# A two-layer decoder trunk on one core: a refitted table of transfer durations and a larger delay for the inverse in the ordering pass, and the S5 tables loaded in two transfers

## The chip, the core and the metric
The kernel runs on one core of one Trainium2 chip. The metric is the device time of one execution in microseconds. "PE" is the matrix engine, "DVE" the vector engine, "ACT" the scalar engine, "POOL" GpSimd, and "SP" the engine that issues most DMA transfers here.

## The reference
A decoder trunk of two post-norm layers on x (1024 positions, 1024 features), in fp32, with 256 memory tokens:
```python
for i in range(2):
    if i == 0:
        mix, xq = gdn_mixer(x, ...)      # gated DeltaNet, 8 heads of 128
    else:
        mix, xq = s5_mixer(x, ...)       # 64 groups, 64 complex states each, GLU
    cross = memory_attention(xq, mem, w_kv[i])          # 4 heads
    h = concatenate([mix, cross], -1) @ w_o[i]
    x = layer_norm(ALPHA * x + h, ln1_g[i], ln1_b[i])
    f = square(relu(x @ mlp_w1[i])) @ mlp_w2[i]         # 1024 -> 4096 -> 1024
    x = layer_norm(ALPHA * x + f, ln2_g[i], ln2_b[i])
```
In the DeltaNet, each chunk of 64 positions solves a unit triangular system (I + A) X = [V, K exp(g)], where A is the strictly lower part of beta K K^T times a decay. Then a state S of 128 x 128 per head goes from chunk to chunk: v_new = u - w S, o = (q exp(g)) S + (q k^T decay) v_new, S = S exp(g_last) + k_dec^T v_new. The S5 mixer runs, per group, a complex diagonal recurrence over the positions.

## The kernel before
**Products.** Large products are made as three matmuls in the type fp32r (`mm3`, L386 to L391): each operand is split into a high part (a cast on ACT, L368 or L857) and a low part (a subtraction on DVE, L369 or L858). A result tile in a trace row is named after its use: wi and wz are projections of the input with xT (x, transposed) and the weights wih, wil (or wzh, wzl), loaded raw as wir (wzr) by L359. Raw weight tiles have the tag "raw", of which there are two buffers; `mlp_sums` (L626 to L637) shares them: it loads two blocks of the MLP's first weight (w1r), makes sums and differences of their quarters in place on DVE (L631 to L634) and stores them to wsum in DRAM (L636).

**Layer 0.** Heads are taken one after the other. `gdn_recur` (L1441) runs the recurrence of a head over eight steps of 128 positions: on PE, ks (L1465) and po (L1468) read S; DVE makes R (L1467); PE makes pe (L1471) from R and the inverse iv; ACT copies it to e (L1473); PE makes pS (L1477) and po (L1483) from e; DVE makes the next S (L1482). Each waits for the one before, so the projections and the convolution of a later head (DVE, L1105 to L1117) are woven in as filler.

**The inverse.** The triangular systems of two heads at a time are inverted in four rounds, heads 0/1 to 6/7. `gdn_inverse_` (L1189) inverts small blocks on DVE with products (L1256) and sums (L1258, TENSOR_REDUCE); POOL writes the results to the DRAM tensor t32 (L1268, L1269), a row of the trace named t<-X. `gdn_invert_tiles` (L1271) reads them back through SP, as iv<-t (L1292) and bd<-t (L1295), and completes the inverse with small products on PE (L1279). `self.patient` holds the names of all instructions that `gdn_inverse_` emits.

**After the heads.** `rows` (L2315) loads x for the residual in sixteen DMAs, as y (L2321); then come the output projection, the layer norm (L519, L531), the MLP, and layer 1. S5's `s5_driving` (L2005) loads, per block and half, two table tiles "tab" of [128, 4, 128] on POOL's queue (L2016); `s5_drive` multiplies them at L2059.

**Order.** The kernel is emitted in a plain order and then re-ordered as a whole by `settle` (L58 ff.), a list scheduler over all instructions of PE, ACT, DVE, POOL and SP. It holds a model of time: `price` (L295) gives each instruction how long its engine is busy and how long until its result is there. For a DMA it also gives `moves`, the time on a single modelled DMA server that serves all transfers one after the other; it depends on the size and on k, the shortest contiguous run of either side in bytes (L309, L310). Each PE instruction's due time is its place in PE's own program; for the others it is counted back from those that wait for them (L185 to L190). An instruction of DVE in `self.patient` gets a later due time (L191 to L193), so that others may go ahead of it. Among the instructions that are ready, the earliest due goes first. So a change of a price moves instructions on all engines. The order that comes out is fixed in the program; no time is decided on the chip.

Of the kernel before, what the change touches and what calls it, by code (L numbers as in the profile page):

```python
# [16 lines left out]
P = 128  # L17
# [13 lines left out]
class Trunk:  # L31
# [26 lines left out]
    def settle(self, first, last, reach=0.0, ahead=15.0, passes=1, margin=0.0, late=0.0, hold=1e3, stay=(0.0, 0.0), turn_=0.0):  # L58


        E = mybir.EngineType
# [83 lines left out]
        for x in range(n):  # L145
            for nm in uses(ins[x]) & before:
                if self.home.get(nm, "s")[0] == "ps":
                    k = nm, ins[x].engine
# [3 lines left out]
            for y in deps[x]:  # L152
                if ins[y].engine != ins[x].engine:
                    k = y, ins[x].engine
# [10 lines left out]
        for x in range(n):  # L165
            for nm in fresh[x]:
                t = held.setdefault(self.home[nm][:2], [])
# [13 lines left out]
        for _ in range(passes):  # L181
            due, now = [0.0] * n, 0.0
# [7 lines left out]
                    due[x] = min([due[y] for y in after[x] + next_[x]] + [now + 50.0]) - lag - cost[x][1]  # L190
            for x in range(n):  # L191
                if ins[x].name in self.patient and ins[x].engine == E.DVE:
                    due[x] += 15.0  # L193


            slots, turn = {}, {}
# [24 lines left out]
            while len(order) < n:  # L221
                first_ = None
                drift = free[E.PE] - due[turns[head]] if head < len(turns) else 0.0
                for e in names:
                    pick = None
                    for x in open_[e]:
# [13 lines left out]
                        k = (0, due[x] + other, r, x) if r <= free[e] + 0.1 else (1, r + other, due[x], x)  # L240
# [5 lines left out]
                r, x = first_[1:]  # L246
                e = ins[x].engine
                busy, length, moves = cost[x]
# [21 lines left out]
                for nm in fresh[x]:  # L270
                    t = self.home[nm][:2]
# [23 lines left out]
    def price(self, i, big):  # L295

        E = mybir.EngineType
        if i.opcode == "DMACopy":
            def run(ap):
                k = 1  # L300
                for s, c in reversed(ap):
                    if s != k:
                        break
                    k *= c
                return 4 * k

            q = [x.bass_ap.ap for x in (i.ins[0], i.outs[0])]
            size, k = 4e-3 * math.prod(c for s, c in q[1]), min(run(a) for a in q)
            moves = size / (300 if k >= 2048 else 230 if k >= 512 else 150 if k >= 256 else 90 if k >= 128 else 40)  # L309
            return (0.33 if i.engine != E.Pool else 0.65), 1.6 + size / 300 + (0.0 if k >= 512 else 0.7), moves  # L310
        if i.engine == E.PE:
            if i.ins[0].dtype == F32R:
                return 0.014 + 0.416e-3 * big, 0.39 if big > 256 else 0.29, 0
            wide = max(math.prod(c for s, c in x.bass_ap.ap[1:]) for x in i.ins)
            if i.is_transpose:
                return 0.11, 0.27, 0
            part = i.outs[0].bass_ap.ap[0][1] / P
            if part < 1:
                return 0.01 + 1.66e-3 * max(wide, 64) * part, 0.35, 0
            return 0.01 + 1.66e-3 * wide, 0.39, 0  # L320
        q = [x.bass_ap.ap[-1] for l in (i.ins, i.outs) for x in l if getattr(x, "bass_ap", None) is not None]
        slow = 1.65 if any(s > 1 and c > 1 for s, c in q) else 1.0
        scalars = any(math.prod(c for s, c in x.bass_ap.ap[1:]) == 1 for x in i.ins if getattr(x, "bass_ap", None) is not None) and big > 1
        if i.engine == E.Activation:
            bank = self.home.get(i.ins[0].bass_ap.tensor.name, "s")[0] == "ps"
            if i.opcode == "TensorCopy":
                t = max((0.05 if bank else 0.096) + 0.84e-3 * big * slow, 0.29)
            else:
                t = (0.08 if bank else 0.125) + 0.8e-3 * big + (0.22 if len(i.outs) > 1 else 0.0) + (0.07 if scalars else 0.0)
            return t, t + 0.1, 0  # L330
        if i.engine == E.Pool:
            t = 0.02 + 0.87e-3 * big if i.opcode == "Memset" else 0.5 if big < 2 else 1.0 if big < 8 else 0.17 + 2.1e-3 * big
            return t, 4.4 if 1 < big < 8 and i.opcode != "Memset" else t + 0.05, 0
        wide = sum(c > 1 for x in i.ins if getattr(x, "bass_ap", None) is not None for c in [math.prod(c for s, c in x.bass_ap.ap[1:])])
        if getattr(i, "is_tensor_tensor_scan", False):
            return 2.46e-3 * big, 2.46e-3 * big + 0.08, 0
        t = 0.07 + (0.53e-3 if i.opcode == "TensorScalarPtr" and wide < 2 else 1.04e-3) * big * slow + (0.06 if scalars and i.opcode == "TensorScalarPtr" else 0.0)
        return t, t + 0.08, 0
# [1666 lines left out]
    def s5_driving(self, m):  # L2005

        out = []
        for b in range(2):
            gs = slice(4 * b, 4 * b + 4)
            G1 = self.s5_load("G1", "h1", self.g1d[m, :, gs])  # L2010
            c, q = (2 * m + b) % 8, m // 4
            tabs = []
            for x in range(2):
                t = self.tile("h2", [P, 4, P], F32, "tab")
                src = self.tabd[1:3, c, q] if x else self.tabd[0, c, q].unsqueeze(0).to_broadcast([2, 64, 4, P])
                self.nc.gpsimd.dma_start(t.rearrange("p g t -> p (g t)"), src.rearrange("k p g t -> k p (g t)"))  # L2016
                tabs.append(t)
            out.append((G1, tabs))
        return out
# [462 lines left out]
```

## Time and profile before
| | |
|---|---|
| runs before | 2498.58, 2492.67, 2499.19 us; median 2498.58 |
| the profiled execution | 2495.45 us |
| its span | 2493.7 us |
| PE busy | 2461.7 us |
| mean granted clock of PE | 0.998 |
| transfers | 424.12 MB, DMA engines busy in the mean 46.2% with SP's queue and 7.3% with POOL's |

The span runs from the first to the last instruction of the profile; the rest of the execution's time lies around it. A busy PE is one with a matmul in flight: matmuls are pipelined, so a row's duration (0.39 us for 512 columns) is longer than the distance to the next row. In a timeline's row stand the start and the duration in us, the engine, line, operation, output <- input, shapes, and the count; brackets give the engine's idle time before it and what ended it. SPq is the queue side of SP. Times on POOL are rough.

### The profile page before, as it was taken

How to read it: one execution, taken by the hardware profiler on the slowest of the kernel's cores; microseconds unless marked ns; L12 is line 12 of the kernel's file. 1: busy time of each engine (PE TensorE's matmuls, PEld its weight loads, DVE VectorE, ACT ScalarE, POOL GpSimd, SP SyncE). 2: the span in 40 equal slices, each digit the busy share in tenths (PEclk: the TensorE clock that was granted, in tenths of full speed). 3: DMA queues.
4: the chain of work that ended last, by engine and by line, in shares of the span. 5: the costliest groups of instructions: out<-in, count | busy, mean ns of one | idle time of the engine just before them, and what ended most of it. 6: DMA issues, size and time to landing. Idle time of an engine off the chain costs nothing. (4 is left out here: it accounts for less than half of the span.)

```text
span 2493.7 us, 37109 instructions
## 1 busy us (share of the span) xinstructions
PE 2461.7 (99%) x12589; PEld 2043.5 (82%) x12589; DVE 1928.7 (77%) x3629; ACT 1385.4 (56%) x3091; POOL 283.7 (11%) x405
## 2 busy tenths in 40 slices
PE   9999999999999999999999999999999999999998
PEld 7888888887787888788888888888887888888886
DVE  7776868685889987879988856683988655588777
ACT  7766677755557575554444255662466555544443
POOL 1111212110001011312120122100010000000001
PEclk9999999999999999999999999999999999999999
DMA  6544445556335665587455499874137544673422
GB/s 205 130 121 147 134 142 146 167 157 209 106 125 176 212 225 182 175 281 250 140 168 158 141 247 224 206 257 153 57 124 240 176 154 152 208 275 101 148 88 98
DMA packets 292047, 424.12 MB, mean 170 GB/s; under 512 B 120032, under 2 KB 137392, under 8 KB 291856
## 3 DMA queue, kind: packets, MB, share of 16 engines
q1 hardware_dynamic: 257520, 370.40, 46.2%
q0 software_dynamic: 31744, 46.76, 7.3%
q10 hardware_dynamic: 2592, 4.59, 0.5%
q8 instruction: 99, 1.62, 0.3%
q14 instruction: 92, 0.75, 0.1%
HBM read 285.74 MB, written 135.76 MB: 169 GB/s over the span
## 5 line engine op out<-in xcount | busy, mean ns | idle before, releaser
L389 PE MATMUL q<-wkh,hkh 128*128 128x512 f32 x784 | 306.0, 390 | 0.0
L390 PE MATMUL q<-wkl,hkh 128*128 128x512 f32 x784 | 305.7, 390 | 0.0
L391 PE MATMUL q<-wkh,hkl 128*128 128x512 f32 x784 | 305.3, 389 | 0.0
L857 ACT CAST wkh<-wr 128x512 fp32r<-128x512 f32 x168 | 104.9, 624 | 238.0 <-PE q L390 156.5
L389 PEld LDWEIGHTS q<-wkh,hkh 128*128 128x128 f32 x784 | 147.2, 188 | 31.7 <-ACT wkh L857 1.0
L391 PEld LDWEIGHTS q<-wkh,hkl 128*128 128x128 f32 x784 | 147.2, 188 | 30.5
L390 PEld LDWEIGHTS q<-wkl,hkh 128*128 128x128 f32 x784 | 147.2, 188 | 30.0
L858 DVE TENSOR_TENSOR wkl<-wr,wkh 128x512 fp32r<-128x512 f32 x168 | 115.8, 689 | 64.0 <-issue 50.9
L389 PE MATMUL wi<-xTh,wih 128*128 128x512 f32 x376 | 151.8, 404 | 1.6 <-ACT wih L368 1.6
L391 PE MATMUL wi<-xTh,wil 128*128 128x512 f32 x376 | 150.0, 399 | 0.3 <-DVE wil L369 0.3
L390 PE MATMUL wi<-xTl,wih 128*128 128x512 f32 x376 | 150.1, 399 | 0.0
L512 POOL TENSOR_TENSOR mv<-mv,mhalf 128x1 f32<-128x1 f32 x32 | 32.1, 1004 | 981.0 <-DVE mv L506 936.4
L858 DVE TENSOR_TENSOR hkl<-hr,hkh 128x512 fp32r<-128x512 f32 x196 | 134.2, 685 | 2.8 <-ACT hkh L857 2.7
L857 ACT CAST hkh<-hr 128x512 fp32r<-128x512 f32 x196 | 121.3, 619 | 4.0 <-DMA hr<-hd 4.0
L389 PE MATMUL o<-ow,ok 128*128 128x512 f32 x256 | 101.4, 396 | 1.2 <-ACT ok L1733 1.0
L391 PE MATMUL o<-ow,ok 128*128 128x512 f32 x256 | 101.5, 396 | 0.2
L390 PE MATMUL o<-ow,ok 128*128 128x512 f32 x256 | 100.2, 391 | 0.1
L850 DVE TENSOR_TENSOR y<-q,y 128x512 f32<-128x512 f32 x136 | 88.0, 683 | 0.0
L389 PEld LDWEIGHTS wi<-xTh,wih 128*128 128x128 f32 x376 | 71.2, 189 | 15.2 <-ACT wih L368 1.8
L391 PEld LDWEIGHTS wi<-xTh,wil 128*128 128x128 f32 x376 | 71.2, 189 | 14.4 <-DVE wil L369 1.0
L390 PEld LDWEIGHTS wi<-xTl,wih 128*128 128x128 f32 x376 | 71.3, 190 | 12.5
L1733 ACT CAST ok<-os 128x512 fp32r<-128x512 f32 x56 | 34.8, 623 | 54.8 <-PE o L391 41.1
(619 smaller groups left out, 7287.7 us busy)
## 6 DMA issues: line engine op xcount, KB each, us to landing
hr<-hd SPq DMA_DIRECT2D x212, 256.0 KB, 2.7
wr<-in_w_dram SPq DMA_DIRECT2D x56, 512.0 KB, 5.0
hd<-u SPq DMA_DIRECT2D x100, 256.0 KB, 2.2
w1r<-in_w_dram SPq DMA_DIRECT2D x48, 512.0 KB, 3.7
hd<-hid SPq DMA_DIRECT2D x60, 256.0 KB, 2.1
hd<-p SPq DMA_DIRECT2D x60, 256.0 KB, 2.6
w1r<-in_w_dram SPq DMA_DIRECT2D x48, 256.0 KB, 3.2
wir<-in_w_in_dram SPq DMA_DIRECT2D x23, 512.0 KB, 4.3
```

Source lines behind the costliest of these rows:

```text
L389: mm(ps, a[0], b[0], start=start, stop=False, skip_group_check=onto)
L390: mm(ps, a[0], b[1], start=False, stop=False, skip_group_check=onto)
L391: mm(ps, a[1], b[0], start=False, stop=stop, skip_group_check=onto)
L512: nc.gpsimd.tensor_tensor(mv[:, 3:4], mv[:, 2:3], self.mhalf[:, 0:1], op=ALU.pow)
L850: V.tensor_tensor(o, bank[t], o, op=ALU.add)
L857: nc.scalar.copy(hi, s)
L858: nc.vector.tensor_tensor(lo, s, f32(hi), op=ALU.subtract)
L1733: nc.scalar.copy(hi, s)
```

## The change
Three edits. In `settle`, the later due time of the inverse's DVE instructions is 20 us instead of 15. In `price`, the modelled rate of a transfer by its contiguous run gets new steps: runs from 1024 bytes on count as 330 (before: 300, from 2048 on), 512 as 280 (230), 256 as 210 (150), 128 as 150 (90), 64 as 90 and shorter ones as 45 (40), and the fixed part for short runs is 0.3 us instead of 0.7. In `s5_driving`, each table tile comes in two transfers of 64 partitions instead of one of 128. The first tile's two halves are the same table, the second's are two tables that lie one behind the other.
```diff
             for x in range(n):
                 if ins[x].name in self.patient and ins[x].engine == E.DVE:
-                    due[x] += 15.0
+                    due[x] += 20.0
...
-            moves = size / (300 if k >= 2048 else 230 if k >= 512 else 150 if k >= 256 else 90 if k >= 128 else 40)
-            return (0.33 if i.engine != E.Pool else 0.65), 1.6 + size / 300 + (0.0 if k >= 512 else 0.7), moves
+            moves = size / (330 if k >= 1024 else 280 if k >= 512 else 210 if k >= 256 else 150 if k >= 128 else 90 if k >= 64 else 45)
+            return (0.33 if i.engine != E.Pool else 0.65), 1.6 + size / 330 + (0.0 if k >= 512 else 0.3), moves
...
                 t = self.tile("h2", [P, 4, P], F32, "tab")
-                src = self.tabd[1:3, c, q] if x else self.tabd[0, c, q].unsqueeze(0).to_broadcast([2, 64, 4, P])
-                self.nc.gpsimd.dma_start(t.rearrange("p g t -> p (g t)"), src.rearrange("k p g t -> k p (g t)"))
+                for k in range(2):
+                    self.nc.gpsimd.dma_start(t[64 * k:64 * k + 64], self.tabd[x * (1 + k), c, q])
                 tabs.append(t)
```
The number of instructions stays the same on PE, DVE, ACT and SP; POOL issues 32 DMAs more. The order changes mostly from 40 to 80 us (keys and values of the memory), from 150 to 620 us (the heads) and from 750 to 870 us (the layer norm), as the trace of before has these places. From there on it is nearly the same.

The first place is on PE, in the recurrence of head 6 (560 to 568 us of the trace), from pe_1091 on. pe, pS, po and ks are the recurrence's products; wi_1117 is the projection of the next head's values or keys with the weights wih_1115 and wil_1116; iv_1065 is the first product of the inverse with what came back from DRAM. Before:
```order
L1471 MATMUL pe_1091_6373<-R_1089_6360,iv_914_5420 128x128
L390 MATMUL wz_1090_6363<-xTl1_20_149,wzh_1047_6126 128x512
L391 MATMUL wz_1090_6363<-xTh1_19_148,wzl_1048_6127 128x512
L1477 MATMUL pS_1094_6396<-e_1092_6375,kdl_1002_5929 128x128
L1483 MATMUL po_1055_6170<-e_1092_6375,mix_288_1774 128x128
L1465 MATMUL ks_1098_6415<-S_1095_6398,kT_32_323 128x128
L1468 MATMUL po_1055_6170<-S_1095_6398,gb_968_5758 128x128
L1471 MATMUL pe_1101_6429<-R_1099_6417,iv_914_5420 128x128
L1483 MATMUL po_1055_6170<-e_1102_6431,mix_288_1774 128x128
L389 MATMUL wi_1117_6475<-xTh0_17_146,wih_1115_6471 128x512
L390 MATMUL wi_1117_6475<-xTl0_18_147,wih_1115_6471 128x512
L391 MATMUL wi_1117_6475<-xTh0_17_146,wil_1116_6472 128x512
```
And now, where fourteen more matmuls of wi follow, between ks, po, pe and po, before iv_1065 comes:
```order
L1471 MATMUL pe_1091_6373<-R_1089_6360,iv_914_5420 128x128
L390 MATMUL wz_1090_6363<-xTl1_20_149,wzh_1047_6126 128x512
L391 MATMUL wz_1090_6363<-xTh1_19_148,wzl_1048_6127 128x512
L389 MATMUL wi_1117_6475<-xTh0_17_146,wih_1115_6471 128x512
L390 MATMUL wi_1117_6475<-xTl0_18_147,wih_1115_6471 128x512
L1477 MATMUL pS_1094_6396<-e_1092_6375,kdl_1002_5929 128x128
L1483 MATMUL po_1055_6170<-e_1092_6375,mix_288_1774 128x128
L391 MATMUL wi_1117_6475<-xTh0_17_146,wil_1116_6472 128x512
L389 MATMUL wi_1117_6475<-xTh0_17_146,wih_1115_6471 128x512
L390 MATMUL wi_1117_6475<-xTl0_18_147,wih_1115_6471 128x512
```
The recurrence's steps stood side by side and had three matmuls of wi behind them before iv_1065; now nineteen stand between them.

The second place is SP's queue at the same time, from the storing of the sums on. Before:
```order
L2321 DMA y_1218_6991<-in_x_dram 128x512
L636 DMA wsum_125<-w1r_1105_6448 128x1024
L2321 DMA y_1219_6992<-in_x_dram 128x512
L2321 DMA y_1220_6993<-in_x_dram 128x512
L636 DMA wsum_125<-w1r_1104_6446 128x1024
L359 DMA wir_1114_6469<-in_w_in_dram 128x1024
L1353 DMA Dq_1082_6333<-ded_115 128x512
L1124 DMA gb_1083_6335<-gcd_304 128x512
L1292 DMA iv_8_107<-t32_118 32x8x32 x2
```
And now:
```order
L636 DMA wsum_125<-w1r_1105_6448 128x1024
L359 DMA wir_1114_6469<-in_w_in_dram 128x1024
L636 DMA wsum_125<-w1r_1104_6446 128x1024
L359 DMA wir_1138_6605<-in_w_in_dram 128x1024
L2321 DMA y_1218_6991<-in_x_dram 128x512
L2321 DMA y_1219_6992<-in_x_dram 128x512
L2321 DMA y_1220_6993<-in_x_dram 128x512
L1353 DMA Dq_1082_6333<-ded_115 128x512
L359 DMA wzr_1162_6736<-in_w_in_dram 128x1024
L1124 DMA gb_1083_6335<-gcd_304 128x512
L1292 DMA iv_8_107<-t32_118 32x8x32 x2
```
The weights wir and the sums moved ahead of the loads of y, and the next two raw weights ahead of the reading of the inverse.

The third place is ACT at 53 to 59 us, among the casts of the memory's value weights wvh and the scaling of keys (kd) and decays (D), as the difference of the two orders:
```order
 L368 CAST wvh_114_870<-wvr_113_868 128x1024
 L1545 CAST kv_90_725<-mk_106_806 128x256
-L368 CAST wvh_117_888<-wvr_116_886 128x1024
-L1545 CAST kv_90_725<-mk_110_839 128x256
 L1164 ACTIVATE kd_47_436<-kt_46_422,scr_5_97 128x128 x4
 L1134 ACTIVATE D_45_416<-D_45_416,scr_5_97 128x128 x4
 L1167 ACTIVATE D_45_416<-D_45_416,scr_5_97 128x128 x4
-L1179 COPY pkd_43_407<-NT_42_401 32x128
+L368 CAST wvh_117_888<-wvr_116_886 128x1024
```
One cast of a weight moved behind twelve activations.

## The prediction
> **What bounds the kernel now.** I read the page's busy row first. PE works for all but 32.0 us of the span (2493.7 less 2461.7), so no other engine sets the length: a change can only remove or add idle time of PE, or of its clock.
> ```profile
> span 2493.7 us, 37109 instructions
> PE 2461.7 (99%) x12589; PEld 2043.5 (82%) x12589; DVE 1928.7 (77%) x3629; ACT 1385.4 (56%) x3091; POOL 283.7 (11%) x405
> ```
> Next the windows: a stretch in which PE is the bound, which gives the pitch of a 512-wide matmul (100 us by 443 = 0.226 us), and three at the end of the DeltaNet heads, where it isn't (columns: length; PE, PEld, DVE, ACT, POOL busy; granted clock; DMA share; GB/s).
> ```profile
> 2200.00:2300.00 100.00, 100.00 (x443) 82.84 (x442) 79.90 (x129) 42.42 (x74) 0.00 (x0) 1.00 0.53 177
> ...
> 545.00:555.00 10.00, 10.00 (x57) 8.59 (x56) 10.00 (x19) 5.28 (x19) 0.00 (x0) 1.00 0.01 2
> 555.00:565.00 10.00, 8.37 (x45) 6.37 (x43) 7.77 (x18) 3.48 (x10) 4.44 (x5) 1.00 0.92 284
> 565.00:575.00 10.00, 8.11 (x53) 5.50 (x55) 3.73 (x5) 3.27 (x6) 0.00 (x0) 0.66 0.72 201
> ```
> I call 560 to 575 the knot: PE idles 1.63 + 1.89 = 3.5 us there and is then granted 0.66 of its clock, which in 10 us costs up to 3.4 us more. The window ahead of it has the DMA at 0.01, the next one at 0.92. The timeline says why (PE first, then ACT, DVE and SP; the bracket is the idle time ahead of a row and what ended it):
> ```profile
> 566.14 0.53 PE L389 MATMUL wi<-xTh,wih 128*128 128x512 f32 x1 [1.62 <-ACT wih L368]
> 567.40 0.79 PE L391 MATMUL wi<-xTh,wil 128*128 128x512 f32 x1 [0.30 <-DVE wil L369]
> 568.35 0.47 PE L1279 MATMUL iv<-iv,nm 64*64 64x64 f32 x2 [0.16 <-DMA iv<-t]
> 574.33 0.62 PE L1279 MATMUL iv<-zi,bd 64*64 64x64 f32 x13
> ```
> ```profile
> 565.05 1.03 ACT L368 CAST wih<-wir 128x1024 fp32r<-128x1024 f32 x1
> ```
> ```profile
> 555.14 1.28 DVE L1258 TENSOR_REDUCE X<-pr 128x32 f32<-128x512 f32 x2
> 557.53 0.69 DVE L634 TENSOR_TENSOR w1r<-w1r 128x512 f32<-128x512 f32 x1
> 566.12 1.23 DVE L369 TENSOR_TENSOR wil<-wir,wih 128x1024 fp32r<-128x1024 f32 x1 [2.99 <-ACT wih L368]
> ```
> ```profile
> 554.39 0.33 SPq L2321 DMA_DIRECT2D y<-in_x_dram  x1
> ...
> 559.18 0.33 SPq L359 DMA_DIRECT2D wir<-in_w_in_dram  x1
> ...
> 566.53 0.81 SPq L1292 DMA_DIRECT2D iv<-t  x2
> ```
> The weights of the next projection (wir) start only at 559.18, behind the row loads y in SP's queue and behind the sums of L634 that hold the raw buffer. They are cast at 565.05, and PE waits 1.62 us for that at 566.14. Meanwhile the inverse goes from DVE (last reduce ends at 555.14 + 1.28 = 556.4) through DRAM to PE at 568.35.
>
> **The change part by part.** *The knot.* Ahead of wir the order now puts the sums L631 to L634, and SP issues wsum, wir, wsum, wir before the three y loads; the y loads keep their place in time, since they wait for DVE anyway. So wir can be in the chip before 554, its cast follows the first e (about 551 to 561 instead of 565.05), and PE gets 19 matmuls of wi between the recurrence steps instead of 3. This removes the 1.62 us and covers the waits of the recurrence, which are most of the other 1.9. The price stands on DVE: L633, L1357, L634, S and one L1114 go ahead of the last reduces, four wide operations at the 0.60 to 0.66 us from one start to the next, and one at 0.26: 2.7 us. The inverse is complete at 559.1 instead of 556.4. From there the rows of the way through DRAM count (median us from issue to landing last; then the landing of this round's writes, and POOL's last write of it):
> ```profile
> t<-X POOLq DMA_DIRECT2D x16, 32.0 KB, 3.2
> iv<-t SPq DMA_DIRECT2D x16, 32.0 KB, 2.0
> ...
> bd<-t SPq DMA_DIRECT2D x32, 32.0 KB, 3.0
> ```
> ```profile
> DMA to landing us min/median/max: 7.5/7.5/7.5
> ```
> ```profile
> 559.76 0.69 POOL L1268 DMA_DIRECT2D t<-X  x1
> ```
> POOL's last write moves to 559.76 + 2.7 = 562.5. With the usual 3.2 us it lands at 565.7, with this round's 7.5 (taken beside a DMA share of 0.92) at 570.0. I take 4.2: the y loads now lie earlier than the writes, but the load of wzr is freed by wil at about 562.6 and falls beside them. Then iv<-t is issued at 566.7 and lands at 568.7; bd<-t follows after the two issues of iv (0.81), its four take 0.4 us each (1.6), and the last lands 3.0 us on, 572.1. PE arrives at iv_1065 near 567.4, having waited some 0.8 us for wil, and waits again until 568.7. It starts iv_1070 at 572.1 instead of 574.33 (which had no wait: PE came there late), 2.2 us sooner, with 24 matmuls of wi done instead of 14 (10 x 0.226 = 2.3 us of work that is then not left). That is 4.5 us; the products of iv_1093, which had two matmuls of wi and two transposes ahead of them (0.8 us), now wait bare, some 1.0 us. Term: -3.5. Each us of landing is a us of the term: -4.5 at 3.2 us, about -0.2 at 7.5; the best case is that all of 3.5 + 3.4 us goes, -6.9.
>
> The granted clock in that window was 0.66 although no idle stretch on PE was longer than the 1.62 us shown. The Trainium skill, "TensorE: Matmul & The Clock Gate", section "HAM oscillation — how this bites in real kernels", gives as its rule that PE must have no idle gaps over about 3.4 us; this trace does not agree, since gaps under half of that came with a clock of 0.66. By that rule the gaps of 0.8 and 1.3 us that I expect would cost no clock, and the term would be what it is. By the row they can cost up to 3.4 us again; the sum counts part of this as kept, by going through iv_1070's time and not through the whole -6.9.
>
> *The two rounds before it* (heads 2 to 5). Here too about 2.6 us of convolution go ahead of the last reduce, and PE's products of the inverse stand only five or six rows later (1.2 us).
> ```profile
> 427.97 0.69 DVE L1258 TENSOR_REDUCE X<-pr 128x32 f32<-128x512 f32 x1
> ...
> 433.57 0.81 SPq L1292 DMA_DIRECT2D iv<-t  x2
> ```
> ```profile
> 433.64 0.50 PE L389 MATMUL wz<-xTh,wzh 128*128 128x512 f32 x1 [0.41 <-ACT vT L1112]
> 437.30 0.68 PE L1279 MATMUL iv<-iv,nm 64*64 64x64 f32 x16
> ```
> iv is issued by 434.4, lands 2.0 us later at 436.4, and is used at 437.30 without a wait: 0.9 us of cover and 1.2 of later use against 2.6 of delay leave 0.5 us per round. Waits such as the 0.41 get filler ahead of them, two or three in each round. I put the sum of both rounds at +0.3, between -1 (fillers alone) and +2.5 (longer landings).
>
> *Memory keys and values, 53 to 59 us.* Here one weight cast on ACT moves behind twelve small activations, which takes it from 53.27 to about 56.7, and its low part on DVE follows:
> ```profile
> 53.27 1.05 ACT L368 CAST wvh<-wvr 128x1024 fp32r<-128x1024 f32 x1
> ...
> 56.66 1.30 ACT L1167 ACTIVATE D<-D,scr 128x128 f32<-128x128 f32 x4
> ```
> ```profile
> 57.06 0.39 PE L389 MATMUL mv<-wvh,memh 128*128 128x512 f32 x1
> ```
> The matmul of 57.06 has no wait now; with the cast at 56.7 + 1.05 = 57.8 it waits 0.7 to 1.0 us. The low part of the weight before it moves behind one wide DVE operation (0.6 us), and PE waits for it already. If both counted, +1.6; PE's fill of other products may take some: +1.2, between 0.3 and 2.5.
>
> *The layer norm after the heads.* One or two small adds move behind y, for which PE waits five times:
> ```profile
> PE xt L531 <- DVE y L519: 2.0, 5, 0.7
> ```
> -0.6, between -1.2 and 0.
>
> *The S5 tables.* Sixteen pairs of loads become twice as many transfers of half the size (issue time in ns and first and last start; the use; the landing):
> ```profile
> L2016 POOL DMA_DIRECT2D tab<-tabd x32: 787/816/866, 1366.6 to 1579.2; - x32
> ```
> ```profile
> L2059 DVE TENSOR_TENSOR t<-r,tab x16: 667/681/686, 1448.5 to 1617.9; 128x512 f32<-128x512 f32 x16
> ```
> ```profile
> DMA to landing us min/median/max: 9.0/11.9/18.6
> ```
> At most 32 more issues of 0.82 us, 26 us on a POOL that works 283.7 of 2493.7. From the first load to its first use lie 82 us, from the last to its last 39, and landing takes at most 18.6; even 10 us more would be covered. 0, and a gain is as little possible, since no one waits for them. The order after 870 us hardly changes elsewhere.
>
> **The sum:** -3.5 + 0.3 + 1.2 - 0.6 = -2.6 us. The profiled execution took 2495.45 us with a span of 2493.7; that is 3.1 below the median of the three runs shown, 2498.58 (2492.67 to 2499.19). Set on the mean of the four, 2496.5, the sum gives 2493.9, called 2494.
>
> **The rivals.** About 0.3% (7.5 us) is what can be told from no change, so faster is below 2491.1 and slower above 2506.1.
> - *No net change.* The knot's writes land after 7 us again, and the term is -0.2; with the others' +0.9 the time is 2497. For: that round's 7.5 us, and wzr falls beside the writes. Against: 3.2 us is the median of sixteen. Chance 0.25.
> - *The knot dissolves.* PE is fed throughout, the clock isn't halved: -6.9, the fillers give -1, the layer norm -1.2, the memory part +0.3: -8.8, 2488. For: the wir load, the only long wait in it, is gone. Against: the inverse, late by 2.7 us, had 0.16 us to spare. Chance 0.25.
> - *The late inverse decides, and it gets slower.* Each round's inverse is complete 2.6 us later; if its writes land over 2 us later than the usual 3.2, PE stands bare at iv in all three rounds. Price: 2.5 + 2.5 us in the first two, no gain in the third, and a clock of 0.66 over 10 us after each of the two new gaps, 6.8; with the memory part's 1.2 that is +13, 2509.5; without the clock +6, 2503. For: 0.9 us of cover in the row of 437.30. Against: there the DMA was not as full. Chance 0.10.
>
> **How the numbers follow.** The forecast has the remaining 0.40; its own range is 2490.5 to 2497.5 (landings from 3.2 to 7.5, the others at their ends in part). Below 2491.1 lie nearly all of the second rival (0.24) and 0.06 of the forecast: 0.30. Above 2506.1 lies the third with its clock and some spread: 0.09. Within: 0.61. The range of 8 in 10 goes from 2485 to 2503: the spread of runs of one kernel here (6.5 us) lies on every case.
>
> **What would show it.** Right: no row of wih with a wait at L389 over 0.5 us in the knot; the y rows behind two wir rows on SP; the last reduce about 2.7 us later; the clock in the ten us after it above 0.66; casts wvh after the D rows near 57, and a wait of 0.7 to 1 us at mv; tab rows twice as many, with no wait on them. Wrong: PE's wait for iv<-t over 3 us in any round; a wait of DVE on tab; idle time of PE outside these places that changes by more than 2 us.

## The result and the profile after
The changed kernel takes 2509.45 us (median of 6 runs, 2506.50 to 2513.56), before 2498.09 (6 runs, 2492.67 to 2499.19): a ratio of 1.0055, 95% interval 1.0045 to 1.0064. It is slower by 11 to 16 us. 2494 was predicted, with a range of 2485 to 2503.

The page of the changed kernel begins:
```profile
span 2507.0 us, 37177 instructions
PE 2464.0 (98%) x12589; PEld 2043.7 (82%) x12589; DVE 1924.1 (77%) x3629; ACT 1382.6 (55%) x3091; POOL 281.2 (11%) x437
```
PE now idles 43.0 us instead of 32.0, and that is most of the 13.3 us by which the span has grown. The windows of the knot come some 11 us later than before, because so much had been lost by then (columns as in the windows of the prediction):
```profile
555.00:565.00 10.00, 10.00 (x56) 8.57 (x55) 10.00 (x18) 5.38 (x19) 0.00 (x0) 1.00 0.55 201
565.00:575.00 10.00, 10.00 (x55) 8.45 (x54) 9.97 (x21) 4.63 (x8) 4.06 (x5) 1.00 0.51 137
575.00:585.00 10.00, 9.33 (x106) 7.66 (x104) 3.30 (x7) 5.36 (x15) 0.00 (x0) 1.00 0.71 209
590.00:600.00 10.00, 7.08 (x38) 5.39 (x38) 3.55 (x8) 2.48 (x10) 1.81 (x2) 0.83 0.18 38
```
The knot is gone from its place: PE idles 0.67 us from 555 to 585 and has its full clock. Another hole has opened behind it, at 590, with 2.92 us of idle time and a clock of 0.83. From 557 to 617 PE idles 4.2 us in all, against 3.5 us from 545 to 605 before. What PE waits for in the new hole (the rows with a wait), and at the other new places:
```profile
591.19 0.30 PE L1279 MATMUL iv<-iv,nm 64*64 64x64 f32 x2 [0.52 <-DMA nm<-ntf]
591.99 0.45 PE L1279 MATMUL iv<-iv,nm 64*64 64x64 f32 x8 [0.51 <-DMA nm<-ntf]
594.99 0.27 PE L1279 MATMUL iv<-iv,nm 64*64 64x64 f32 x2 [1.88 <-DMA nm<-ntf]
```
```profile
265.27 0.49 PE L1465 MATMUL ks<-S,kT 128*128 128x128 f32 x2 [1.22 <-DVE S L1482]
369.52 0.49 PE L1465 MATMUL ks<-S,kT 128*128 128x128 f32 x2 [1.18 <-DVE S L1482]
385.63 0.66 PE L1371 MATMUL vt<-ident,vT 128*128 128x128 f32 x4 [1.69 <-DVE mix L1363]
532.04 0.49 PE L1465 MATMUL ks<-S,kT 128*128 128x128 f32 x2 [1.31 <-DVE S L1482]
1467.58 0.80 PE L2078 MATMUL py<-s5t 128*128 128x128 f32 x2 [4.11 <-DMA s5t<-zd]
```
These are waits all along the heads, and one of 4.11 us in the S5 mixer, at 1467.

To see where the 13 us came from I laid PE's two timelines against each other: each matmul counts as the median distance from its kind to the next row, and where both kernels have done the same sum of work, the difference of the two times is the lag. (My own working from all 12589 rows of each trace; times are before's.)

| stretch | lag at its end, us | gained or lost there |
|---|---|---|
| to 70: memory keys and values | +1.5 | +1.5 |
| 70 to 540: heads 0 to 5 | +11.8 | +10.3 |
| 540 to 575: the knot | +5.2 | -6.6 |
| 575 to 600: behind the knot | +10.0 | +4.8 |
| 600 to 660: the last head | +12.2 | +2.2 |
| 660 to 1090: layer norm, MLP | +10.4 | -1.8 |
| 1400 to 1475: S5's front | +15.1 | +4.7 |
| the rest | +13.6 | -1.5 |

**How a wait of ks comes about.** The DVE timelines around 261 to 265, after and then before:
```profile
263.68 0.69 DVE L1385 SCALAR_TENSOR_TENSOR thz<-thz,zc 128x512 f32<-128x512 f32 x1
264.28 0.68 DVE L1222 TENSOR_REDUCE X<-pr 128x64 f32<-128x512 f32 x1
264.87 0.34 DVE L1482 SCALAR_TENSOR_TENSOR S<-S,scr,pS 128x128 f32<-128x128 f32 x1
```
```profile
261.05 0.34 DVE L1482 SCALAR_TENSOR_TENSOR S<-S,scr,pS 128x128 f32<-128x128 f32 x1
...
262.76 0.68 DVE L1385 SCALAR_TENSOR_TENSOR thz<-thz,zc 128x512 f32<-128x512 f32 x1
```
S stands behind wide work that before stood behind it. ACT and DVE were also late, because earlier in their order something had waited for a transfer to land. Three rows of the changed kernel show it; before has no row with a wait for a landing on ACT or DVE from 240 to 268:
```profile
252.44 0.63 ACT L1356 ACTIVATE gb<-gb 128x512 f32<-128x512 f32 x1 [2.80 <-DMA gb<-gcd]
253.11 0.69 DVE L1357 TENSOR_TENSOR gb<-gb,qT 128x512 f32<-128x512 f32 x1 [1.50 <-ACT gb L1356]
384.89 0.69 DVE L1363 TENSOR_TENSOR mix<-qk,Dq 128x512 f32<-128x512 f32 x1 [2.67 <-DMA Dq<-ded]
```
The late landing of gb holds ACT for 2.80 us and, through it, DVE for 1.50; DVE waits 0.67 us once more, for a cast, at 255.76, and from there to S at 264.87 no row of it has a wait. PE's 1.69 us at 385.63 end with the mix of the third row, which had waited 2.67 us for Dq. The wait at 369.52 has no landing wait on ACT, DVE or PE in the 15 us ahead of it, so not every one of these waits comes about in this way. The waits for landings between 240 and 660 us (engine, line, waited for, us in total, times, longest), before and then after:
```profile
ACT gb L1356 <- DMA gb<-gcd: 5.8, 5, 1.8
```
```profile
DVE mix L1363 <- DMA Dq<-ded: 0.2, 1, 0.2
```
```profile
ACT gb L1356 <- DMA gb<-gcd: 13.0, 7, 3.2
```
```profile
DVE mix L1363 <- DMA Dq<-ded: 7.9, 4, 2.7
```
I call the sum of all such rows (ACT, DVE and PE, 240 to 660 us) the landing waits: 11.1 us before, 38.1 after. They are not lost one for one, since most of them are on engines with time to spare. PE itself waits 17.0 us in this stretch, 7.6 before. Of the 17.0, 4.2 end with a landing (0.4 before), and 2.4 more with a mix that had just waited for Dq.

**S5's front.** The load of zd and the first matmul that uses it (first and last start; the landing), before and then after:
```profile
L2031 POOL DMA_DIRECT2D s5t<-zd x7: 1315/1324/1344, 1446.6 to 1593.1; - x7
...
DMA to landing us min/median/max: 10.0/12.3/13.7
```
```profile
1464.76 0.38 PE L2078 MATMUL py<-s5t 128*128 128x128 f32 x2
```
```profile
L2031 POOL DMA_DIRECT2D s5t<-zd x7: 1332/1341/1351, 1456.6 to 1608.5; - x7
...
DMA to landing us min/median/max: 11.0/13.3/13.6
```
Before, PE came to py 18.2 us after the issue. Now it comes 6.9 us after it (1467.58 - 4.11 - 1456.6), for a load that takes 11. One py had moved ahead by 48 rows of PE, from behind the projection wu to ahead of it. By the new price this load lands 1.6 + 512/330 + 0.7 = 3.9 us after its issue, if no other transfer is ahead of it in the plan.

### The profile page after: what moved, and what is told of

Read it like the earlier page. It is cut to its first block, busy times and chain, and to the rows that moved or that the text cites. A ratio compares the mean times of both kernels' runs of the same rounds, so it can differ in the third digit from the quotient of the medians.

```text
span 2507.0 us, 37177 instructions
## 1 busy us (share of the span) xinstructions
PE 2464.0 (98%) x12589; PEld 2043.7 (82%) x12589; DVE 1924.1 (77%) x3629; ACT 1382.6 (55%) x3091; POOL 281.2 (11%) x437
## 3 DMA queue, kind: packets, MB, share of 16 engines
q0 software_dynamic: 17920, 46.65, 6.8%
q8 instruction: 99, 1.62, 0.3%
```

## The experiments
In each run the landing waits are summed as above; "before" is before's time in runs on the same chip. All but e3 give the program another order in the heads. The first four take the change apart.

**e1, patience alone.**
```diff
-                    due[x] += 15.0
+                    due[x] += 20.0
```


> Only the later due time of the inverse (20 us instead of 15); table and S5 loads as before. Theory T (the loss comes from the new table of durations, by which the order puts uses of a transfer ahead of its landing): this order has the knot at 560 to 575 dissolved too, so -6 us there, part of it given back just behind it where the filler is now missing (+3 to +5), little else: 2 to 3 us below before, no S5 wait. Theory P (the loss is the late inverse): the +5 at head 7's inverse and +5 at the rounds of heads 2 to 5, less the knot's 6: 3 to 6 us above before.


2489.65 us, before 2497.84: ratio 0.9973 (0.9959 to 0.9987). Landing waits 7.8. Its windows in the place of the knot and PE's rows with a wait there:
```profile
565.00:575.00 10.00, 6.83 (x84) 5.75 (x83) 1.70 (x4) 3.84 (x12) 0.87 (x1) 0.89 0.61 173
575.00:585.00 10.00, 9.55 (x86) 7.90 (x85) 6.24 (x14) 7.54 (x31) 1.50 (x1) 0.94 0.53 120
```
```profile
568.76 0.90 PE L1279 MATMUL iv<-iv,nm 64*64 64x64 f32 x16 [0.86 <-DMA iv<-t]
571.97 0.59 PE L1279 MATMUL iv<-zi,bd 64*64 64x64 f32 x13 [2.31 <-issue]
578.10 0.85 PE L1279 MATMUL iv<-iv,x 64*64 64x64 f32 x16 [0.45 <-ACT x L1328]
```
The waits for weights are gone, but PE now waits at the inverse (2.31 us at the products that read bd, with no releaser shown): from 545 to 605 it idles 3.6 us, as long as before (3.5). What is smaller there is the loss of clock: the clock is at one half for 3.41 us instead of 6.83. By the lag, 3.6 us are gained from 540 to 620, the rest in small steps elsewhere. Faster, by more than theory T gave, and against theory P.

**e2, the table alone.** Patience 15, S5 loads as before.
```diff
-            moves = size / (300 if k >= 2048 else 230 if k >= 512 else 150 if k >= 256 else 90 if k >= 128 else 40)
-            return ..., 1.6 + size / 300 + (0.0 if k >= 512 else 0.7), moves
+            moves = size / (330 if k >= 1024 else 280 if k >= 512 else 210 if k >= 256 else 150 if k >= 128 else 90 if k >= 64 else 45)
+            return ..., 1.6 + size / 330 + (0.0 if k >= 512 else 0.3), moves
```


> Only the new table of transfer durations; 15 us of patience, S5 loads as before. Theory T: nearly the whole loss, 9 to 14 us above before, with the 4 us wait of py for s5t<-zd, and waits of mix for Dq in the heads. Theory P: 4 to 6 us above before (the S5 wait and the memory keys alone), the waits at the heads near those of before.


2519.39 us, before 2497.84: 1.0087 (1.0069 to 1.0105). Landing waits 45.2; py waits for zd (3.9 us). More than the whole loss is in the table, and more than the 9 to 14 us that theory T gave it.

**e3, the split S5 loads alone.**
```diff
-                src = self.tabd[1:3, c, q] if x else self.tabd[0, c, q].unsqueeze(0).to_broadcast([2, 64, 4, P])
-                self.nc.gpsimd.dma_start(t.rearrange("p g t -> p (g t)"), src.rearrange("k p g t -> k p (g t)"))
+                for k in range(2):
+                    self.nc.gpsimd.dma_start(t[64 * k:64 * k + 64], self.tabd[x * (1 + k), c, q])
```


> Only the S5 tables in two transfers. The order on PE is that of before. Theory T and P: within 1 us of before, no wait of py on s5t<-zd. Theory Q (the 32 further issues on POOL's queue delay the load of zd behind them): the 4 us wait of py is here, +4 us.


2495.66 us, before 2497.84: 0.9993 (0.9983 to 1.0002). No wait of py: theory Q falls, the split costs nothing.

**e4, patience and table, no split**: the diffs of e1 and e2 together.


> Patience and table together, S5 loads as before: the changed kernel without the split. Theory T and P: 10 to 14 us above before, as the changed kernel, py's wait of 4 us included (the load of zd lands after 10 us or more in both kernels). Theory Q: 4 us less than the changed kernel.


2516.94 us, before 2497.84: 1.0074 (1.0051 to 1.0096), py waits 4.1 us. Four to five us above the range expected; its interval and the changed kernel's overlap. Theory Q, which had it 4 us faster than the changed kernel, falls again.

**e5, the changed kernel with one landing corrected.** In the plan only:
```diff
                     length = served - r + late
+                    if e == mybir.EngineType.Pool and moves > 1.5:
+                        length += 8.0
```


> The changed kernel, with 8 us more in the plan for the landing of the 512 KB loads on POOL's queue. On PE it moves one matmul alone: the first py goes back from ahead of the projection wu to behind it. Theory T (the shortened durations place that use before its load has landed): py's wait of 4.1 us is gone and the kernel is 4 to 5 us faster than the changed one, about 9 above before. Rival (the wait is only moved: something else in the S5 front ends last): within 2 us of the changed kernel.


2504.95 us, before 2499.38: 1.0026 (1.0015 to 1.0037), against 1.0055 of the changed kernel. The first py, at 1472.5, has no wait:
```profile
L2080 PE MATMUL py<-s5t x112: 270/275/276, 1472.5 to 1622.0; 128*128 128x128 f32 x112
```
By the lag from 1400 to 1475 (4.7 us in the changed kernel, 0.3 here), 4 to 5 of the lost us are this one matmul's place. The two ratios differ by 7 us, so some of it lies outside S5: the profiled execution of the changed kernel has its clock at one half for 3.41 us each from 596.6, 641.0 and 1467.0, that of e5 only at its very end. Two later products of py (L2081) now wait 1.0 us in all for H.

**e6, patience and split with the old table**: the diffs of e1 and e3 together.


> Patience 20 and the split S5 loads, with the table of before. Theory T: the sum of the two runs alone, 0.9973 x 0.9993 = 0.9966, 8 to 9 us below before and faster than both kernels. Rival (the split only spreads noise): as patience alone, 6.7 below before.


2492.42 us, before 2499.38: 0.9974 (0.9964 to 0.9985). As patience alone; the split adds nothing.

**e7 and e8, the table in two.** e7 has only the first line of e2's diff (`moves`, the rates), e8 only the second (the other terms).


> Of the table only the new rates by row length; the durations' other terms, patience and S5 loads as before. The first py stays behind wu. Theory T1 (the rates do it): 12 us or more above before. Theory T2 (the lower lengths do it): within 5 us of before. Rival R (any change of the order costs, whatever its sense): 8 to 12 us above, in the heads.

> Of the table only the other terms (330 instead of 300, 0.3 instead of 0.7 us for short rows); rates, patience and S5 loads as before. The first py stays behind wu. Theory T1: within 5 us of before. Theory T2: 12 us or more above before. Rival R: 8 to 12 us above, in the heads.


e7: 2521.46 us, before 2499.38: 1.0094 (1.0070 to 1.0117), landing waits 58.1, the highest of all runs. Its first rows of PE's waits:
```profile
PE ks L1465 <- DVE S L1482: 9.1, 10, 3.1
PE iv L1279 <- DMA iv<-t: 4.5, 3, 3.4
```
e8: 2499.77 us, 1.0009 (0.9995 to 1.0023), landing waits 17.0, although it moves about as many rows of PE as e7. The rates do it. The rates set how long a transfer holds the one server of the plan, through which all transfers go, so they decide when the next one is taken to start.

**e9 and e10, the rates in two**, short rows (e9) and long ones (e10), in the place of before's line:
```diff
+            moves = size / (300 if k >= 2048 else 230 if k >= 512 else 210 if k >= 256 else 150 if k >= 128 else 90 if k >= 64 else 45)
...
+            moves = size / (330 if k >= 1024 else 280 if k >= 512 else 150 if k >= 256 else 90 if k >= 128 else 40)
```


> Of the rates only the tiers under 512 bytes (210, 150, 90, 45 instead of 150, 90, 40); patience and the rest as before. Theory T: ACT, DVE and PE wait for landings in the heads (240 to 660 us) between 20 and 40 us in all (11 before, 57 with all rates), and the kernel is 6 to 14 us above before. Rival R (any new order costs about 10 us): 8 to 12 us above, whatever the waits for landings are.

> Of the rates only the tiers from 512 bytes on (330 from 1024, 280 from 512, instead of 300 from 2048 and 230 from 512). Theory T: the rest of the 23 us that all rates cost: 8 to 16 us above before, waits for landings in the heads 20 to 40 us. If the short rows alone were the cause: within 4 us of before.


e9: 2509.22 us, before 2497.44: 1.0043 (1.0028 to 1.0058), landing waits 43.7; its time fits theory T and rival R alike. e10: 2510.43 us, 1.0049 (1.0030 to 1.0067), landing waits only 15.8: theory T had 20 to 40. Its profiled span is 15.1 us longer than before's; by the lag 6.6 of them have come by 620 us, and the rest comes after 1400, with a wait for a weight's cast there:
```profile
PE wu L389 <- ACT wuh L368: 3.4, 1, 3.4
```
PE has before's order from 1400 to 1620, and the same late cast stands in traces of kernels that cost nothing (last section). So a good part of e10's loss may not come from what the new rates moved.

**e11 and e12, the other way**, both with patience 20: slower rates (e11), longer other terms (e12).
```diff
+            moves = size / (240 if k >= 2048 else 180 if k >= 512 else 110 if k >= 256 else 70 if k >= 128 else 30)
...
+            return ..., 2.2 + size / 250 + (0.0 if k >= 512 else 1.1), moves
```


> The rates changed the other way (240, 180, 110, 70, 30 instead of 300, 230, 150, 90, 40), with patience 20. It moves more rows of PE than the changed table. Theory T (only shortened durations cost): waits for landings in the heads at or below before's 11 us, and the time within 4 us of patience alone, 6.7 below before. Rival R: 5 to 15 us above before.

> The other terms changed the other way (2.2 us and size over 250, 1.1 us for short rows, instead of 1.6, 300 and 0.7), with patience 20. Theory T: waits for landings in the heads at or below before's 11 us, time within 4 us of patience alone. Rival R: 5 to 15 us above before.


e11: 2534.76 us, before 2497.44: 1.0155 (1.0136 to 1.0173), with landing waits of 5.5. e12: 2500.37, 1.0014 (1.0004 to 1.0023), landing waits 5.7. Theory T as it stood falls: the slowest kernel of the study hardly waits for landings, and e12 lost the gain of patience (theory T had it within 4 us of e1). The PE of e11 waits for DVE and ACT, for instance
```profile
PE pe L1471 <- DVE R L1467: 3.6, 4, 1.8
PE ks L1465 <- DVE S L1482: 3.4, 5, 1.8
PE wi L389 <- ACT wih L368: 2.6, 3, 1.6
PE q L389 <- ACT wkh L857: 2.5, 1, 2.5
```
that is, for the recurrence and for casts of weights. It looks as if a plan that takes transfers for slow brings the loads in too late or too far apart, but no run tests that.

**e13, a table that is 1% off.** Patience 15.
```diff
+            moves = size / (303 if k >= 2048 else 232 if k >= 512 else 152 if k >= 256 else 91 if k >= 128 else 40)
```


> The table of before with rates higher by about 1% (303, 232, 152, 91, 40), patience 15: durations as good as unchanged, yet 645 matmuls stand elsewhere in the heads (1097 with the new table). Theory T: within 4 us of before, waits for landings in the heads about 11 us. Rival R: 8 us or more above before.


2498.86 us, before 2497.19: 1.0004 (0.9993 to 1.0014), landing waits 13.6. Rival R, that any new order costs, falls here and in e8: rows of PE (645 here, by the count in the expectation) may stand elsewhere at no cost.

**e14 and e15, the new table with more time to land.** e5's kernel with another value of `late`, which the plan adds to the landing of every transfer, 1.7 (e14) and 2.7 us (e15) instead of 0.7:
```diff
-        self.settle(..., margin=0.2, late=0.7, stay=(0.7, 4.0), turn_=0.04)
+        self.settle(..., margin=0.2, late=1.7, stay=(0.7, 4.0), turn_=0.04)
```


> The kernel of e5 (changed kernel, load of zd late in the plan) with 1.7 instead of 0.7 us added to the landing of every transfer in the plan. Theory T: waits for landings in the heads fall from 38 to below 20 us, and the time from 5.6 us above before to before's or below. Rival R: 5 us or more above before.

> As e14 with 2.7 us. Theory T: waits for landings in the heads at most before's 11 us, time at or below e14's. Rival R: 5 us or more above before; by slower rates, which cost 37 us without waits for landings, it could also overshoot: 10 or more above.


e14: 2498.75 us, before 2497.19: 1.0008 (0.9996 to 1.0019), landing waits 23.2 instead of e5's 38.0. e15: 2501.29, 1.0012 (1.0003 to 1.0021), landing waits 3.5. With a us more for every landing e5's 1.0026 falls by some 4.5 us; a second us takes the landing waits away without a further gain. Of T's two numbers for e14 both were missed by a little: the time came out 2 us above before, the landing waits 3 above 20. Rival R's 5 us or more did not come.

**e16, patience 20 and the old table, 1.7 us for landing**: the diffs of e1 and e14 together.


> Patience 20 alone (2489.7, 6.7 below before) with 1.7 instead of 0.7 us, table of before. Its waits for landings are 8 us already. Theory T: nothing to gain, within 3 us of patience alone. Rival R: the order of e1 is lost, 0 to 10 us above before.


2502.73 us, before 2497.19: 1.0016 (1.0005 to 1.0028), landing waits 6.8. The gain of e1 is gone, as rival R had it: this plan, which already waited little for landings, loses by longer ones. With 0.7 us the new table (e5) lies 0.0053 above the old one (e1), with 1.7 us (e14 and e16) 0.0008 below. Most of that change is the old table's loss (0.0043), not the new one's gain (0.0018).

**e17 and e18, patience once more**: 20 with e13's table, and 25 with the old one.
```diff
-                    due[x] += 15.0
+                    due[x] += 25.0
```


> The table that is 1% off, with patience 20 instead of 15. If patience gains by its mechanism (weights ahead of the rows y on SP, knot gone): 4 to 8 us below before, as e1. If e1's gain was the luck of one order: within 3 us of e13, that is of before.

> Patience 25, table of before. If patience gains by its mechanism: 3 to 9 us below before, since the knot's fix needs no more than 20. If the late inverse becomes the last to arrive: above e1 by 3 us or more. By luck: anywhere within 5 us of before.


e17: 2493.59 us, before 2497.83: 0.9986 (0.9973 to 1.0000), 4 to 5 us below e13 and 3.5 below before, which lies between its two expectations. e18: 2500.60, 1.0011 (0.9997 to 1.0026). At 20 patience gains with both tables, 4 to 7 us; at 25 the gain is gone, and the trace shows where most of it went:
```profile
574.32 0.47 PE L1279 MATMUL iv<-iv,nm 64*64 64x64 f32 x2 [4.36 <-DMA iv<-t]
```
```profile
575.00:585.00 10.00, 8.50 (x97) 7.62 (x98) 3.11 (x6) 3.49 (x13) 0.00 (x0) 0.58 0.48 110
```
The inverse is the last to arrive: 4.36 us at iv, and a clock of 0.58 from 575 to 585. By the lag, e18 lies 3.1 us behind before at 620, where e1 is 3.8 ahead.

## Why the prediction was wrong
The prediction read the right places but not all of them, and it priced the table at what moved in sight of known waits. The step that failed is the sum's term for the rounds of heads 2 to 5, +0.3: it stood for all of the heads ahead of the knot, where 10.3 us were lost. Second, the order after 870 us was put at nothing, where one use lost 4.7. The last of its signs of being wrong did appear: idle time of PE outside the places that it names.

- *The knot* (-3.5, at best -6.9): right in its mechanism, and in its place the gain was larger, -6.6. No wait of wih is left, wir stands ahead of y, and the clock is full. The last reduce came at 569.5, about 1.3 us later than before with the lag of 11.8 taken off, instead of 2.7; the waits at iv are 0.20 and 0.43 us. But the sum ended at iv_1093. Behind it, at 575 to 600, 4.8 us were lost, which leaves -1.8, about what the shorter half clock is worth (3.41 us of it instead of 6.83); the idle time was moved, not removed: the matmuls of wi that fill the recurrence now were the cover of head 7's inverse before. The loads of nm, behind those of bd on SP, land too late for a PE that comes sooner with nothing between (the rows of 591 to 595, and a clock of 0.83). Filler that is moved is missing where it stood.
- *"The two rounds before it"* (+0.3, -1 to +2.5): here it failed. I looked only at the inverse's way in these rounds, and took the rest of the heads for unchanged. In the heads up to 540 us 10.3 us were lost, where PE now waits for the recurrence's S and for mix. The waits at iv<-t are short (1.3 us in all, of three). The table alone costs 21.6 us (e2), its rates alone 22.1 (e7); the one-per-cent table, which moves 645 rows, costs nothing. So it was neither the late inverse nor the moving as such. In place of the +0.3 stands an order in which loads such as gb and Dq are used before they have landed; that this carries the loss is in part argued (below).
- *Memory keys and values* (+1.2): +1.5, with waits of 1.13 and 0.53 us at mv, about as expected. *The layer norm* (-0.6): about -1.8 in the whole stretch to 1090.
- *The S5 tables* (0): right, e3 and e6. The transfers land sooner than I took them to (below).
- *"The order after 870 us hardly changes elsewhere"*: wrong by one matmul; a few other rows move too, with no lag to be seen. Its place costs 4.1 us of waiting, in e2 and e4 too (3.9 and 4.1), which is got back in e5. A matmul that moves by 48 rows moves by 11 us of PE; among 12589 rows it does not show in a count.
- *The rivals.* The third named nearly the time that was measured, 2509.5, but its mechanism, the late inverse as the last to arrive in every round, is not what happened, so the agreement is chance. It is real all the same, one step further: at patience 25 (e18). The rule of the Trainium skill by which the prediction weighed the clock is spoken of below.

What is shown: the loss is the table's (e1 to e4), in its rates (e7, e8); 4 to 5 us of it are one use placed ahead of its landing (e5); and a us more for every landing takes most of e5's remaining loss away (e14), though the same us costs the old table's plan 11 us (e16). With 0.7 us it goes with landing waits that rise from 11 to between 37 and 58 us (changed kernel, e2, e4, e7), where tables that cost nothing keep 14 to 17 (e13, e8). Up to the end of the heads the two go together in the runs with patience 15 (the lag by the working above, at 660 us; one profiled execution each):

| run | e13 | e8 | e10 | e2 | e9 | e7 |
|---|---|---|---|---|---|---|
| landing waits, us | 13.6 | 17.0 | 15.8 | 45.2 | 43.7 | 58.1 |
| lag at 660, us | 0.7 | 5.5 | 6.6 | 12.6 | 16.0 | 26.6 |

That these waits carry the loss of the heads is argued from this and from the rows shown above, not shown wait by wait. Three plans that take transfers for slower, with patience 20, do not follow it: with landing waits of 5.5 to 6.8 us the lag is 26.7 (e11), 5.8 (e12) and 5.0 (e16), where e1 has -3.8 with 7.8. What stays open: why they lose the gain of patience or more, whether the 12 us of e10 are the new rates' (half of it or more comes after 1400, in PE's old order), and which waits for landings are harmless (e14 still has 23 us). That the settings of the ordering pass were tuned to the old numbers, so that any large change of a price loses, is a rival that no run tests. No rule came out that gives the time from the table.

The best kernel of the study is before with patience 20 alone: 2489.65 us, 0.9973 of before.

## What to carry to other kernels
When a change touches the prices of a list scheduler, every use of a transfer is up for review, not the places that waited before: compare the new distance from issue to use with the landing in the trace, transfer by transfer, above all for the long landings (12 us here, where the plan had 4). A filler that is drawn into one hole opens the next one behind it, so carry the sum on to the point where both orders have done the same work. And a table refitted to be "truer" can cost more than it gives: take the edits of a change apart first, since here one of three was worth -7 us and another +22.

## What the runs showed of the hardware
**Split transfers landed sooner.** One load of a table (256 KB, two blocks of 64 partitions) took 816 ns of issue and 11.9 us to land (median). Each of its halves takes:
```profile
L2016 POOL DMA_DIRECT2D tab<-tabd x64: 522/522/576, 1377.0 to 1597.6; - x64
...
DMA to landing us min/median/max: 2.3/6.1/12.0
```
A half carries half the bytes, so the fair comparison is the pair: from the issue of the first half to the landing of the later one it takes 7.1 us (median, from the trace's landings) against 11.9. The queue's packets fall from 31744 to 17920 at nearly the same bytes (46.76 and 46.65 MB). The Trainium skill, "DMA: Bandwidth & Descriptors", section "Rules for kernel authors", says that a transfer whose outermost dimension has fewer than 16 entries is confined to at most as many engines, naming a leading broadcast as an example; the undivided load had an outermost dimension of two. The shorter landing agrees with it; how many engines took part is not shown here.

**The clock did not follow the longest gap.** Before, a longest gap of 1.62 us (3.5 in all) came with 0.66 in the ten us after; here one of 1.88 us (2.9 in all at 591 to 595) with 0.83, in e1 one of 2.31 us with 0.89 and 0.94 in the two windows, in e18 one of 4.36 us with 0.58. The rule of the Trainium skill that the prediction weighed ("TensorE: Matmul & The Clock Gate", section "HAM oscillation — how this bites in real kernels", no gaps over about 3.4 us) fits the last; the other three lost clock below it.

The ten-us means hide how the clock goes: in the clock record of these traces it is whole but for stretches at one half, of 3.41, 6.83 or 10.24 us, and one at the end of each span. Before and then after:
```profile
566.50:573.30 6.80, 6.05 (x26) 3.97 (x25) 2.12 (x4) 2.19 (x4) 0.00 (x0) 0.50 0.76 196
```
```profile
641.00:644.40 3.40, 3.40 (x12) 2.82 (x11) 0.85 (x2) 1.86 (x8) 0.00 (x0) 0.50 0.87 296
```
The stretch is 3.41 us in e1 (from 572.8) and 10.24 in e18 (from 573.1). The one at 641.0 follows waits of no more than 0.68 and 1.00 us. What sets its length is not shown.

**One order, two times.** With before's order of PE in this stretch and no edit near it, e9 waits in S5's front where before doesn't:
```profile
1519.97 0.50 PE L389 MATMUL wu<-xTh,wuh 128*128 128x512 f32 x1 [0.99 <-ACT wuh L368]
1521.23 0.50 PE L391 MATMUL wu<-xTh,wul 128*128 128x512 f32 x1 [0.52 <-DVE wul L369]
```
Its lag rises by 4 us there. Those of e3 and of e13, whose times are before's, rise by 5, with before's order of PE there. The common sign is a late landing of the weight wur: ACT's cast of it waits 4.0 us for it before, 7.1 in e3, 6.1 in e9, 7.9 in e13, and 8.4 in e10. In e3 the issue of the two stores of yd just ahead takes 4.97 us of SP's time instead of 1.51, where the share of the DMA engines was 1.07 before (1490 to 1500); in e9 it takes 1.77, so these issues are not the common cause:
```profile
1494.11 4.97 SPq L2082 DMA_DIRECT2D yd<-zg  x2
```
```profile
1489.92 1.51 SPq L2082 DMA_DIRECT2D yd<-zg  x2
```
Such stretches may be what spreads the runs of one kernel by 6 us; that was not tried.
